# Two-layer RWKV and attention trunk: the token shift as one product on ScalarE and one multiply-add on VectorE, with two new terms in the planner's VectorE costs

## The chip, the cores and the metric

The program runs on one core of one Trainium2 chip. The metric is the device time of one execution in microseconds. The kernel before took 2802.55 us, the median of three runs (2799.92 to 2806.07).

## The reference

A sequence of 16 learned tokens and 1024 inputs (1040 tokens of width 1024, float32) passes through two layers, each a token mixer and a squared-ReLU MLP between normalizations. Layer 0's mixer is what the change touches. One matrix gives 18 tiles of 128 channels each: r, k and v of RWKV (tiles 0 to 11), the low-rank inputs for decay, rate and gate (12 and 13), and the input of a pooling mixer (14 to 17). Tiles 0 to 13 are shifted in time by a learned share mu of each channel:

```python
y = h @ w_in
ys = y[..., :SHIFT_WIDTH]
prev = jnp.pad(ys, ((0, 0), (1, 0), (0, 0)))[:, :L]
ys = ys + (prev - ys) * mu
...
o = rwkv7_scan(rf, dec, kf, vf, kk, a_h)     # S = S*w + sa (kk a) + v k, token by token
...
diffs.append((c - lag) / cnt - ug)           # moving averages of 2, 4, 8, 16 tokens
...
return jnp.concatenate([o, z], axis=-1) @ w_out
```

Layer 1's mixer is differential attention. It and both MLPs have the same instructions before and after.

## The kernel before, in words

**Stages.** Channels lie on the 128 partitions and tokens along the free axis, in three chunks of 348, 346 and 346 tokens. Each fp32 product is made as three fp32r matmuls of split operands (high by high, low by high, high by low; `mm3`, L363 to L370). The program is: an entry stage (normalization of the input, the projections of tiles 12, 13 and 4), the low-rank stage (`lora`), then a large planned stage with the rest of layer 0's mixer, then the output projection and MLP of layer 0 (`late`), attention, and the second `late`.

**The planned stage** lies between about 80 and 665 us. In it the code doesn't issue instructions; a `Recorder` takes each call down with the tiles it reads and writes (`call` and `keep`, L253 to L307), so every instruction of this stage has line L283 in the profile and is known by its tile names. `call` reckons a cost for each from the engine and the size (L263 to L281). `Flow.order` (L118 to L165) then walks through the tasks as a list scheduler: it keeps a clock for each engine, takes the engine that can start soonest, and on it the ready task with the longest chain of reckoned cost behind it. The result is one fixed order for each of the five queues (PE, VectorE, ScalarE, GpSimd, and SP, which issues the DMAs). On the chip each queue runs in that order, whatever the real durations are.

**What is planned.** For each of four pairs of heads p there is
- `proj`: the projections of the tiles that p needs, with the token shift (`project_c`), stored to DRAM (`yd`);
- `prep`: from these the operands of the chunked scan for 17 chunks of 64 tokens, in groups of two (tiles `q`, `w`, `zb`, `sa`, `sg`; two products called `pss` for norms), stored as `pk` and `ldd`;
- `invert`: 62 dependent VectorE operations on a 68-partition tile (`tm` and `raw`, in widths from 31 to 256 and back to 31), which invert the small triangular blocks of all 17 chunks at once. It loads its operands from `ldd` and an identity `eye`, and stores the result as `xd`, from which `ds` is loaded. All four inverts use the same `raw` tile, so one must have stored its result before the next may load;
- `chain`: the scan over the chunks, in groups of two. A group loads `lt` from `pk`, GpSimd builds `bd` from `ds` and `lt`, PE makes three products into `xs` with ScalarE (`x`, `gb`) and VectorE (`x`, `qq`, `mk`) between them, then the state `S` and the output `ob`; a finish with tiles `ft` writes the result to `ozd` or to `opa`.

Beside them stand `pool` (four moving-average mixers: GpSimd and VectorE on `u`, one product `ps<-u`, stored to `ozd`), `load` (reads `ozd` back and splits it into operands `opa`, one ScalarE cast and one VectorE subtraction per 260-token quarter) and `early` (the first six tiles of the output projection, 432 matmuls `ps<-opa,whi/wlo` of 260 columns, which need the loaded quarters). The list `PLAN` in which the generators are written down gives the order of recording, and so which buffer each takes; it is not changed.

**The token shift before.** `project_c` (L1127 to L1159) multiplies the PSUM sum by the row factor into `ys` on VectorE (L1153), with the last column of the chunk before in column 0. `shift` (L1161 to L1164) then makes the difference of the shifted and the unshifted view and a multiply-add, both on VectorE. Twelve tiles in three chunks go this way: three chunks in the entry stage and 33 in the planned one. `lora` also calls `shift`, for tiles 12 and 13 as a whole.

## Time and profile before

| | before |
|---|---|
| median of three runs | 2802.55 us |
| the profiled execution, its own time | 2802.57 us |
| its span | 2800.8 us |
| PE busy | 2597.9 us (93%) |
| VectorE busy | 2097.3 us (75%) |
| ScalarE busy | 1332.5 us (48%) |
| GpSimd busy | 302.4 us (11%) |

The span is the time from the first to the last instruction in the hardware profile; 1.8 us of the execution lie outside it. Times inside it are given from its start. A "row" is a line of one of the profile's views: a group of instructions by operation and shape, a stretch of the span with the busy time of each engine, a stretch of one engine's instructions in order of time, or who waited for whom. In timelines, square brackets hold the idle time just before an instruction and what ended it. PE is the matmul engine, DVE is VectorE, ACT is ScalarE, POOL is GpSimd. The row "PEclk" and the column of that name give the clock granted to the matmul engine, as a share of full speed.

### The profile page before, as it was taken

The numbers are of one execution on the slowest core, as the hardware profiler recorded it, in microseconds if no ns is written. First come the engines' busy times: TensorE is split into PE (matmuls) and PEld (weight loads), VectorE is DVE, ScalarE is ACT, GpSimd is POOL, SyncE is SP. The second block draws the span as 40 slices with busy tenths as digits, with TensorE's granted clock in tenths as the row PEclk, the third lists the DMA queues.
The fourth block names the chain that finished last, engine by engine and source line by source line (L and its number), as shares of the span: only waits on it lengthen the run. The fifth ranks groups of instructions, "written<-read, shape, count | busy, mean of one in ns | idle before, by whom it ended". The sixth has DMA issues, their size and how long they took to land.

```text
span 2800.8 us, 44525 instructions
## 1 busy us (share of the span) xinstructions
PE 2597.9 (93%) x16822; PEld 2359.1 (84%) x16822; DVE 2097.3 (75%) x3897; ACT 1332.5 (48%) x2727; POOL 302.4 (11%) x404
## 2 busy tenths in 40 slices
PE   7999988599999999999968999999899999999997
PEld 6889887499899999999957899988786788778877
DVE  5469778643987778887785888888648778778887
ACT  5456667243633335433343555655645333443342
POOL 0111333230000000000012232222000000000000
PEclk9999999699999999999988999999999999999998
DMA  4465676554333345443332222222243243544443
GB/s 152 168 204 187 211 222 216 146 162 169 137 114 126 147 177 205 168 137 130 96 127 68 69 64 79 63 67 61 76 160 129 105 165 141 196 174 137 149 160 119
DMA packets 180182, 391.16 MB, mean 140 GB/s; under 512 B 43104, under 2 KB 103904, under 8 KB 167552
## 3 DMA queue, kind: packets, MB, share of 16 engines
q1 hardware_dynamic: 152784, 348.14, 37.5%
q10 hardware_dynamic: 27184, 40.18, 4.1%
q8 instruction: 132, 2.16, 0.3%
q14 instruction: 82, 0.67, 0.1%
HBM read 240.17 MB, written 131.18 MB: 133 GB/s over the span
## 4 chain that ended last, share of the span: by engine, by line
PE 66%; DVE 9%; ACT 3%; issue 2%; DMA 2%; SPq 0%; POOL 0%; DVEq 0%; ACTq 0%
PE bank L681 46%; PE psq L368 2%; PE psq L369 2%; PE psq L370 2%; PE ps L283 2%; PE s L1777 1%; PE xs L283 1%; PE s L1779 1%; PE tr L1823 1%; ACT p L1796 1%; PE bank L723 1%; PE ob L283 1%; PE av L1849 1%; DVE p L1809 1%; DVE ac L758 1%
## 5 line engine op out<-in xcount | busy, mean ns | idle before, releaser
L681 PE MATMUL bank<-opa,wp 128*128 128x260 f32 (+1 forms) x3296 | 656.7, 319 | 6.9 <-DVE wp L772 3.5
L681 PEld LDWEIGHTS bank<-opa,wp 128*128 128x128 f32 x3296 | 517.0, 188 | 57.0 <-DVE wp L772 5.0
L681 PE MATMUL bank<-opb,wp 128*128 128x260 f32 (+1 forms) x1150 | 349.4, 325 | 3.0 <-DVE ac L991 3.0
L283 PE MATMUL ps<-opa,whi 128*128 128x346 f32 (+2 forms) x1008 | 267.9, 328 | 31.9 <-ACT opa L283 20.6
L681 PE MATMUL bank<-opa,hh 128*128 128x260 f32 (+1 forms) x1112 | 239.6, 320 | 7.2 <-DVE hh L772 5.3
L681 PEld LDWEIGHTS bank<-opb,wp 128*128 128x128 f32 x1150 | 217.4, 189 | 22.5 <-ACT opa L1014 3.4
L991 DVE TENSOR_TENSOR ac<-bank,ac 128x520 f32<-128x520 f32 (+1 forms) x256 | 171.1, 690 | 69.6 <-PE bank L681 67.7
L681 PE MATMUL bank<-opa,opb 128*128 128x260 f32 (+4 forms) x1168 | 203.7, 304 | 11.3 <-ACT opb L660 7.3
L283 PEld LDWEIGHTS ps<-opa,whi 128*128 128x128 f32 x1008 | 179.5, 191 | 34.5 <-ACT opa L283 21.1
L681 PEld LDWEIGHTS bank<-opa,hh 128*128 128x128 f32 x1112 | 184.7, 190 | 23.6 <-DVE hh L772 5.8
L681 PEld LDWEIGHTS bank<-opa,opb 128*128 128x128 f32 x1168 | 166.5, 192 | 22.3 <-ACT opb L660 7.7
L681 PE MATMUL bank<-opb,hh 128*128 128x260 f32 (+1 forms) x616 | 179.8, 325 | 0.0
L771 ACT CAST wp<-raw 128x512 fp32r<-128x512 f32 (+1 forms) x138 | 80.4, 584 | 196.7 <-PE bank L681 188.2
L283 PE MATMUL ps<-opa,wlo 128*128 128x346 f32 (+2 forms) x504 | 157.8, 313 | 0.0
L771 ACT CAST wp<-ss 128x512 fp32r<-128x512 f32 (+1 forms) x130 | 76.5, 589 | 165.5 <-PE bank L681 140.7
L1796 ACT ACTIVATE p<-s,m 128x272 f32<-128x272 f32 (+7 forms) x128 | 95.5, 751 | 86.1 <-DVE m L1792 84.4
L681 PE MATMUL bank<-opa,tt 128*128 128x260 f32 (+1 forms) x648 | 130.8, 319 | 2.2 <-ACT opb L1014 2.0
L681 PEld LDWEIGHTS bank<-opb,hh 128*128 128x128 f32 x616 | 116.9, 190 | 9.9
L368 PE MATMUL psq<-opa,wp 128*128 128x346 f32 (+2 forms) x352 | 118.1, 335 | 4.4 <-DVE rp L453 2.6
L353 POOL TENSOR_TENSOR wpx<-raw,wp 128x1024 fp32r<-128x1024 f32 (+1 forms) x14 | 33.9, 2424 | 789.5 <-PE bank L681 745.3
L370 PE MATMUL psq<-opa,wp 128*128 128x346 f32 (+2 forms) x352 | 113.8, 323 | 0.0
L681 PE MATMUL bank<-opb,opb 128*128 128x256 f32 (+4 forms) x456 | 111.4, 308 | 1.4 <-DVE tt L737 1.4
(398 smaller groups left out, 6567.6 us busy)
## 6 DMA issues: line engine op xcount, KB each, us to landing
raw<-in_w_dram SPq DMA_DIRECT2D x64, 1024.0 KB, 4.9
hid<-ac SPq DMA_DIRECT2D x14, 1820.0 KB, 5.8
hid<-ac SPq DMA_DIRECT2D x14, 1792.0 KB
hh<-hid SPq DMA_DIRECT2D x23, 1040.0 KB, 5.2
hh<-hid SPq DMA_DIRECT2D x23, 1024.0 KB, 6.8
pk<-sg ACTq DMA_DIRECT2D x32, 704.0 KB, 3.9
lt<-pk SPq DMA_DIRECT2D x32, 704.0 KB, 4.5
raw<-in_w_qkv_dram SPq DMA_DIRECT2D x24, 512.0 KB, 3.8
```

Of the source, the lines that this page charges most:

```text
L283: one = eng, cost, lambda: fn(*args, **kw), r, w
L353: (lo or nc.gpsimd).tensor_tensor(lw[:, :n], raw[:, :n], hi[:, :n].bitcast(F32), op=ALU.subtract)
L368: nc.tensor.matmul(ps, wh, xh, start=(first and i == 0), stop=False)
L369: nc.tensor.matmul(ps, wl, xh, start=False, stop=False)
L370: nc.tensor.matmul(ps, wh, xl, start=False, stop=(last and i == n - 1))
L681: nc.tensor.matmul(ps, use(x), use(y), start=start and i == j == 0, stop=i == len(ws) - 1 and j == 2, skip_group_check=not start)
L723: nc.tensor.matmul(acc, ones, use(src), start=first, stop=last)
L758: F.dve(NH, lambda mk=mk, k=k: stt(mk, mk, self.gcol(l, 1, k), y, op0=ALU.mult, op1=ALU.mult), r=nm + [("T", 2)], w=nm)
L771: F.act(n, lambda: nc.scalar.copy(use(t[0][:, :n]), src), r=rd, w=[z[0]] + claim)
L991: F.dve(NH, lambda d=d, q=q: tt(sv(d), q, sv(d), op=ALU.add), r=nq + nd, w=nd, ps=True)
L1777: nc.tensor.matmul(out(a, b), st[:, qs], kh[:, a:b], start=True, stop=False)
L1796: nc.scalar.activation(p[:, :L0], S[c][:, :L0], AF.Exp, bias=m2[:, c:c + 1], scale=0.125, accum_out=m2[:, 2 + c:3 + c])
```

## The change

Three edits.

1. In `project_c` the shift of a chunk becomes `z = (1 - mu) * y[1:]` on ScalarE, then `z = mu * y[:-1] + z` on VectorE. `shift` itself stays, for `lora`.
2. A 12-column tile `cmu` with 1 - mu is made once by one VectorE operation. It is a part of the tile `nkk`, whose name it has in the lists below.
3. In the planner's cost of a VectorE operation a `tensor_tensor_scan` is reckoned at 480 elements per us, the others at 960 as before, and 0.06 us is added when any operand is one column wide.

```diff
         elif eng == "DVE":
-            cost = n / 960 + .07 + (.06 if psum else 0.0)
+            cost = n / (480 if op == "tensor_tensor_scan" else 960) + .07 + (.06 if psum else 0.0) + (.06 if any(x.shape[-1] == 1 for x in aps) else 0.0)
...
         if shifted:
-            self.shift(y, mt, W, x[:, off:], x[:, off:])
+            z = x[:, off:]
+            nc.scalar.activation(z, y[:, 1:W + 1], AF.Copy, scale=self.cmu[:, mt:mt + 1])
+            nc.vector.scalar_tensor_tensor(z, y[:, :W], self.par[:, C_MU + mt:C_MU + mt + 1], z, op0=ALU.mult, op1=ALU.add)
...
-            nkk = self.yp.tile([P, 8], F32, name="nkk", bufs=1)
-            self.nkk, self.nka = nkk[:, 0:4], nkk[:, 4:8]
+            nkk = self.yp.tile([P, 20], F32, name="nkk", bufs=1)
+            self.nkk, self.nka, self.cmu = nkk[:, 0:4], nkk[:, 4:8], nkk[:, 8:20]
+            nc.vector.tensor_scalar(self.cmu, self.par[:, C_MU:C_MU + 12], -1.0, 1.0, op0=ALU.mult, op1=ALU.add)
```

Since the planner's costs change and one operation changes its engine, the order of the whole planned stage is a new one on all five queues; behind that stage the order is the same. Three places matter below.

The first is VectorE's queue at the last of the four inverts. Before, the invert's 62 operations (`tm` and `raw`) have only loaded quarters (`opa`) between them, and the first operations of chain 2 (`x_0` on its group `lt_0`, then `qq`, `mk`, and `x_1` of its next group) stand behind the invert's last row:

```order
L283 TENSOR_TENSOR tm_0_794<-raw_724 68x31
L283 TENSOR_TENSOR raw_724<-raw_724,tm_0_794 68x31
L283 TENSOR_TENSOR x_0_807<-lt_0_798,xs_0_803 128x128
L661 TENSOR_TENSOR opb_6261<-raw_724,opb_6261 128x768
L283 TENSOR_TENSOR qq_0_809<-lt_0_798,xs_1_804 128x128
L283 TENSOR_TENSOR mk_759<-lt_0_798,xs_1_804 64x2x64 x2
L283 TENSOR_TENSOR x_1_808<-lt_1_799,xs_0_803 128x256
L283 SCALAR_TENSOR_TENSOR u_2_820<-u_2_820,u_0_818 128x346
```

In the changed kernel the same four stand in the first third of the invert, the first of them behind its tenth operation:

```order
L283 TENSOR_TENSOR x_0_808<-lt_0_799,xs_0_804 128x128
L283 TENSOR_TENSOR opa_72<-yt_0_769,opa_72 128x260
L283 TENSOR_TENSOR tm_0_795<-raw_725 68x156
L283 TENSOR_TENSOR raw_725<-raw_725,tm_0_795 68x6x26
L283 TENSOR_TENSOR tm_0_795<-raw_725 68x175
L283 TENSOR_TENSOR raw_725<-raw_725,tm_0_795 68x7x25
L283 TENSOR_TENSOR tm_0_795<-raw_725 68x192
L283 TENSOR_TENSOR raw_725<-raw_725,tm_0_795 68x8x24
L283 TENSOR_TENSOR tm_0_795<-raw_725 68x207
L283 TENSOR_TENSOR qq_0_810<-lt_0_799,xs_1_805 128x128
L283 TENSOR_TENSOR mk_760<-lt_0_799,xs_1_805 64x2x64 x2
L283 TENSOR_TENSOR x_1_809<-lt_1_800,xs_0_804 128x256
```

Fifteen operations moved in this way from behind the invert into it: of chain 2's first two groups `x`, `qq` and two `mk` each and the four `ft` of its first finish, the last pool's `u`, and two more `opa`.

The second place is SP's queue ahead of that invert. Before, all its loads (`eye` and `ldd`, into `raw`) stand ahead of the four loads of the third invert's result (`ds_0`, which chain 2 needs):

```order
L283 DMA raw_724<-in_eye_dram 64x1024
L283 DMA raw_724<-ldd 16x32x32 x4
L283 DMA raw_724<-in_eye_dram 4x1024
L283 DMA raw_724<-ldd 1x32x32 x4
L283 DMA ds_0_795<-xd 32x16x32 x4
L283 DMA u_0_818<-yd 128x362
```

In the changed kernel they stand ahead of the invert's last five loads, and one quarter's load (`yt`) among the first ones:

```order
L283 DMA raw_725<-in_eye_dram 64x1024
L283 DMA raw_725<-ldd 16x32x32
L283 DMA yt_0_769<-ozd 128x260
L283 DMA raw_725<-ldd 16x32x32 x3
L283 DMA ds_0_796<-xd 32x16x32 x4
L283 DMA raw_725<-in_eye_dram 4x1024
L283 DMA raw_725<-ldd 1x32x32 x4
```

The `ds_0` loads moved up by two places of the queue.

The third place is ScalarE's queue at a pair of projected chunks (the first in the planned stage). Before, it holds the steps of `prep` alone; `q<-pss` is the logarithm of a norm:

```order
L283 ACTIVATE q_0_784<-yl_0_772,nkk 128x64
L283 ACTIVATE q_4_788<-pss_0_792,con 128x128
L283 ACTIVATE q_4_788<-q_4_788 128x128
L283 ACTIVATE sr_1_791<-q_4_788 128x128
L283 ACTIVATE sr_1_791<-yl_3_775,par 128x128
```

In the changed kernel the two products of the shift stand among them:

```order
L283 ACTIVATE q_0_785<-yl_0_773,nkk 128x64
L283 ACTIVATE yt_0_769<-ys_0_771,nkk 128x348
L283 ACTIVATE q_4_789<-pss_0_793,con 128x128
L283 ACTIVATE q_4_789<-q_4_789 128x128
L283 ACTIVATE sr_1_792<-q_4_789 128x128
L283 ACTIVATE yt_1_770<-ys_1_772,nkk 128x346
```

The norm's three steps now stand behind a product that waits for VectorE's `ys`.

## The prediction

> **What bounds the kernel now.** I read the page first: one number for the whole and the slices of the matmul engine.
>
> ```profile
> span 2800.8 us, 44525 instructions
> PE   7999988599999999999968999999899999999997
> PEclk9999999699999999999988999999999999999998
> ```
>
> PE is nearly full in nearly every slice of 70 us, so what counts is PE's idle time. The one deep hole of the planned stage is the eighth slice (490 to 560 us), where the granted clock sinks too. Next, the busy time by stretches of that stage:
>
> ```profile
> core 0: us, PE busy (x) PEld busy (x) DVE busy (x) ACT busy (x) POOL busy (x), PEclk, DMA share, GB/s
> 100.00:480.00 380.00, 346.55 (x2381) 327.31 (x2380) 285.74 (x860) 234.52 (x750) 100.92 (x183) 0.98 0.62 198
> 495.00:542.00 47.00, 15.09 (x73) 12.52 (x73) 32.86 (x89) 8.12 (x24) 8.94 (x12) 0.56 0.48 113
> 542.00:600.00 58.00, 53.55 (x426) 50.95 (x426) 27.52 (x69) 31.53 (x90) 17.47 (x23) 0.97 0.55 168
> 600.00:665.00 65.00, 65.00 (x551) 64.46 (x549) 24.82 (x56) 27.56 (x76) 16.00 (x18) 1.00 0.40 127
> ```
>
> From 100 to 480 us PE idles 33.5 us in 380, in many small waits; from 495 to 542 us it idles 31.9 us in one hole; then 4.5 us in 58, and none to the stage's end. So the stage ends when PE has done a fixed amount of work, and what an edit is worth is the PE idle time that it removes or makes. Whom PE waited for in the first stretch:
>
> ```profile
> PE sa L283 <- DVE sg L283: 10.3, 15, 1.4
> PE sp L283 <- DVE mk L283: 6.0, 4, 3.2
> PE sa L283 <- ACT sg L283: 3.5, 9, 0.9
> ```
>
> And in the hole, PE's timeline:
>
> ```profile
> 506.95 0.58 PE L283 MATMUL ps<-opa,whi 128*128 128x260 f32 x1 [12.08 <-ACT opa L283]
> ...
> 519.49 0.58 PE L283 MATMUL ps<-opa,whi 128*128 128x260 f32 x1 [8.51 <-ACT opa L283]
> ...
> 523.78 0.79 PE L283 MATMUL xs<-x,bd 128*128 128x128 f32 x2 [0.35 <-DVE tm L283]
> 530.29 0.77 PE L283 MATMUL xs<-lt,bd 128*128 128x128 f32 x2 [5.71 <-issue]
> ...
> 539.66 0.36 PE L283 MATMUL ps<-opa,whi 128*128 128x260 f32 x1
> ...
> 543.94 0.61 PE L283 MATMUL xs<-lt,bd 128*128 128x128 f32 x4
> ```
>
> Two kinds of work are left to PE there: `early` products, which wait for loaded quarters, and chain 2 (`xs`), of which only two steps run by 524.6 us. It is held by VectorE, whose timeline is:
>
> ```profile
> 502.57 0.19 DVE L283 TENSOR_TENSOR tm<-raw 68x31 f32<-68x31 f32 x1 [5.10 <-DMA raw<-ldd]
> ...
> 529.79 0.21 DVE L283 TENSOR_TENSOR raw<-raw,tm 68x31 f32<-68x31 f32 x1
> 529.91 0.27 DVE L283 TENSOR_TENSOR x<-lt,xs 128x128 f32<-128x128 f32 x1
> 530.11 0.95 DVE L661 TENSOR_TENSOR opb<-raw,opb 128x768 fp32r<-128x768 f32 x1
> 533.79 0.29 DVE L283 TENSOR_TENSOR qq<-lt,xs 128x128 f32<-128x128 f32 x1 [2.73 <-PE xs L283]
> 533.99 0.58 DVE L283 TENSOR_TENSOR mk<-lt,xs 64x128 f32<-64x128 f32 x2
> 534.71 0.42 DVE L283 TENSOR_TENSOR x<-lt,xs 128x256 f32<-128x256 f32 x1
> 535.05 0.51 DVE L283 SCALAR_TENSOR_TENSOR u<-u,u 128x346 f32<-128x346 f32 x1
> 536.70 0.17 DVE L283 SCALAR_TENSOR_TENSOR ft<-ob,ft 128x16 f32<-128x16 f32 x1 [1.14 <-ACT ft L283]
> 536.91 0.17 DVE L283 SCALAR_TENSOR_TENSOR ft<-ft,ft 128x16 f32<-128x16 f32 x1
> 537.12 0.23 DVE L283 SCALAR_TENSOR_TENSOR ft<-ob,par,ft 128x16 f32<-128x16 f32 x1
> 537.39 0.35 DVE L283 SCALAR_TENSOR_TENSOR ft<-ft,par,ft 128x16 f32<-128x16 f32 x1
> ...
> 539.50 0.85 DVE L283 TENSOR_TENSOR mk<-lt,xs 64x256 f32<-64x256 f32 x2 [0.21 <-PE xs L283]
> 540.38 0.42 DVE L283 TENSOR_TENSOR x<-lt,xs 128x256 f32<-128x256 f32 x1
> 540.72 0.41 DVE L283 TENSOR_TENSOR qq<-lt,xs 128x256 f32<-128x256 f32 x1
> ...
> 546.92 0.94 DVE L283 TENSOR_TENSOR opa<-yt,opa 128x260 fp32r<-128x260 f32 x2 [0.24 <-ACT opa L283]
> ```
>
> The last invert holds VectorE from 502.57 to 530.0 us. The `x` at 529.91 stands behind it, and PE's 530.29 follows from it: the 5.7 us that the row calls "issue" are the wait for the invert. The last pool's `u`, which unlocks further loads for `early`, stands behind it as well.
>
> **Term 1, the shift.** The rows of the operation that goes and of the nearest ScalarE operation of the same form (a scale by a column of `par`):
>
> ```profile
> L283 DVE TENSOR_TENSOR yt<-ys 128x346 f32<-128x346 f32 x22 | 11.9, 539 | 0.9
> L465 ACT ACTIVATE opa<-h,par x24: 568/571/583, 15.3 to 34.7; 128x346 fp32r<-128x346 f32 x16, 128x348 fp32r<-128x348 f32 x8
> ```
>
> 36 differences of 539 ns go: 19.4 us of VectorE. 36 products of 571 ns come: 20.6 us of ScalarE. The multiply-add stays, one small operation for `cmu` is added at the start, under the input's loads. Nearly all of it lies beside PE. In the entry stage three chunks are concerned; ScalarE and VectorE are both ahead of PE there, and I cost it at nothing (if the cover were gone, three times 0.57 us).
>
> In the planned stage 33 of each move. VectorE's load from 100 to 480 us sinks from 285.7 us by 33 times 0.539, 17.8 us or 6%; if PE's 16.3 us of waits for `sg` and `mk` sink by the same share, that is 1.0 us. ScalarE's load rises by 18.8 on 234.5 us, 8%; on the 3.5 us of waits for ScalarE's `sg` that is 0.3 us. A new wait comes with it: a product stands in ScalarE's queue until VectorE has made `ys`, and behind it stand norm steps and evictions (`q`, `sr`, `sg`, `zb`) for which VectorE and PE wait in turn. The bounds: each of the 19 waits for `sg` and `mk` shorter by one difference is 10.2 us of gain; each of the nine waits for ScalarE's `sg` longer by one product is 5.1 us of loss. I take 0.7 us of gain, near the middle, since the new order mixes both kinds of place.
>
> **Term 2, the new order at the last invert.** I take the invert's start as unchanged, 502.57 us. On SP the `ds_0` loads are moved ahead of the invert's last loads:
>
> ```profile
> 490.98 5.03 SPq L283 DMA_DIRECT2D raw<-ldd  x4
> 498.25 0.28 SPq L283 DMA_DIRECT2D raw<-in_eye_dram  x1
> 498.57 2.42 SPq L283 DMA_DIRECT2D raw<-ldd  x4
> 501.03 2.23 SPq L283 DMA_DIRECT2D ds<-xd  x4
> ```
>
> They take 2.23 us to issue, and SP had 2.24 us of idle time (496.01 to 498.25) where they now stand. So they cost nothing there, 2.2 us at most; and they land earlier for chain 2.
>
> The fifteen operations pulled into the invert lengthen it. From the rows above: 0.27 + 0.29 + 0.58 + 0.42 + 0.51 + 0.17 + 0.17 + 0.23 + 0.35 + 0.85 + 0.41 = 4.3 us, and two `opa` 0.9: together 5.2 us. Each could also make the invert wait for a step of PE or ScalarE. Before, 3.9 us passed from `x` to `qq`; now an `opa`, seven steps of the invert and their port waits lie between, some 4 us, so I put that at nothing, with 2 us as its bound. The invert then ends at 535.2 us instead of 530.0. Who waits for that: the store of the result and, behind it on SP, further quarters. Chain 3, which needs the result, comes long after in PE's order, so it costs nothing.
>
> Behind the invert stand two more `opa` (0.9 us) and then `x` of chain 2's third group, which ends at about 536.6 us. Before, that `x` ended at 540.8 us. From there to the fourth group's first product took 3.1 us (543.94), with the second group's `ob` and `sp` and three `early` products between; these are now done by then, which leaves about 1.7 us. So this product runs at 538.3 instead of 543.9 us: 5.6 us gained. By then the changed order has 30 `early` products ahead of it, the old one 21; at 65.00/551 or 118 ns each the nine are 1.1 us. From that place on PE has the same work to the stage's end, 118.6 of 123 us of it busy. Term 2 is 6.7 us of gain. Its bounds: with the 2.2 us on SP and the 2 us of waits, 2.5 us; if the 4.5 us that PE idled from 542 to 600 go as well, 11.2 us.
>
> **The clock in the hole.** After the restart at 530.29 us the matmuls are slow until the row at 539.66, that is for 9.4 us; the stretch was granted 0.56. The changed kernel fills the hole only thinly, so I take the same slow piece after its restart and no term for it. The Trainium skill (TensorE: Matmul & The Clock Gate, Part 1: The HAM clock gate) says that the clock falls to half after an idle window of about 3.4 us and comes back after about as long a busy one. The trace agrees with the half, but not with the short return, if the thin work from 530 us counts as busy. By that rule 6 of the 9.4 us would run at full speed, and the sum would be 3 us lower.
>
> **The sum.** The profiled execution took 2802.57 us, and the median of the runs before is 2802.55, so no correction is needed. 2802.6 - 0.7 - 6.7 = 2795.2; I forecast **2795 us**, 0.27% less. About 0.2%, or 5.6 us, is what a measurement of this kernel can tell from no change. The case's own range, from the bounds of term 2 and half those of term 1, is 2788 to 2802.
>
> **Rivals.** *The loads take the place of the invert.* Since the invert ends 5 us later, SP's store of its result stands 5 us longer ahead of the quarters behind it, and `early` starves after the restart: PE's idle time from 542 to 600 us grows by about what the hole loses. For it: the two long waits at 506.95 and 519.49 are for loaded quarters, not for chain 2. Against: more quarters now stand ahead of that store. It gives 2800 to 2803.
>
> *ScalarE's queue.* The 33 products wait for `ys`, and while one waits, the evictions behind it wait:
>
> ```profile
> L283 DVE TENSOR_TENSOR ys<-ps,rse 128x346 f32<-128x346 f32 x22 | 11.3, 512 | 20.3 <-PE ps L283 20.2
> ```
>
> VectorE itself idled 0.9 us before each of these `ys` for PE. A product placed too early holds ScalarE for that and its own 0.57 us, about 1.5 us. If 10 of the 33 hold an eviction that PE needs, 15 us come and the sum is 2810; it decides against the change from nine on, where the 7.4 us of gain and 5.6 us more are eaten up. For it: PE has only 9% of idle time there, and ScalarE is busy 62%. Against: the planner knows of the dependency and puts other work in front.
>
> *The order is better everywhere.* The reckoned costs are nearer to the real ones, and the hole closes further: by half of its 31.9 us. It gives 2786. For it: chain 2 has three groups free and the pool's `u` runs some 17 us earlier. Against: the quarters' loads are no faster.
>
> *The change moves only what had slack.* Then the hole's gain is lost again before 665 us, 2802; it is told from the first rival only by where PE idles.
>
> **How the numbers follow.** The forecast's case has 0.50, of which 0.36 lies below 2797 and 0.14 within 0.2%. The better order has 0.18 (faster); the two cases without an effect have 0.19 together (same); ScalarE's queue has 0.13, of which 0.12 is slower. That is faster 0.54, same 0.34, slower 0.12. The range of 8 in 10 leaves out the worse half of ScalarE's case and a third of the better order's: 2784 to 2807.
>
> **What would show it.** In the changed profile, VectorE's `x` of 128x128 should start at about 507 us, inside the invert; the invert should last about 33 us instead of 27.4; the fourth group's first `xs` should stand near 538 us; PE's idle time from 100 to 480 us should be 33 us give or take 5; the new ScalarE group `yt<-ys` should have 571 ns. I am wrong if that idle time moves by more than 10 us, if the invert starts more than 3 us later, or if PE has as much idle time from 495 to 600 us as before, 36.4 us.

## The result, and the profile after

The changed kernel takes 2811.93 us, the median of six runs (2808.15 to 2818.0), against 2802.63 for the kernel before (six runs, 2799.92 to 2806.07): a ratio of 1.0033 with a 95% interval of 1.002 to 1.0046. In a second set of runs (`after_again` below) it was 1.0024 (1.0014 to 1.0033). So it is slower by 7 to 9 us, where I had forecast 7.6 us less. The profiled execution is the slowest of the six, 2818.0 us with a span of 2816.2; as before, 1.8 us lie outside.

The first lines of the page, after:

```profile
span 2816.2 us, 44549 instructions
...
PE   7999888599999999999968999999899999999997
...
PEclk9999999699999999999988999999999999999998
```

The slices look as they did; a difference of 0.3% doesn't show in tenths. It has to be looked for between marks. Two marks are in both kernels: the last product of `prep` (`pss`), and the first product of the next stage (`bank`). PE's timeline of before:

```profile
494.48 0.38 PE L283 MATMUL pss<-sr,conb 128*128 128x128 f32 x2
...
666.01 3.86 PE L681 MATMUL bank<-opa,opb 128*128 128x260 f32 x30 [0.93 <-ACT yt L283]
```

And of after, with what PE does in the hole between the two:

```profile
505.38 0.49 PE L283 MATMUL pss<-sr,conb 128*128 128x128 f32 x2 [0.38 <-DVE bo L283]
...
517.80 0.80 PE L283 MATMUL xs<-lt,bd 128*128 128x128 f32 x2 [9.59 <-POOL bd L283]
...
550.76 0.59 PE L283 MATMUL ps<-opa,whi 128*128 128x260 f32 x1 [8.39 <-ACT opa L283]
...
558.65 1.06 PE L283 MATMUL xs<-lt,bd 128*128 128x128 f32 x4
...
677.00 3.89 PE L681 MATMUL bank<-opa,opb 128*128 128x260 f32 x30 [0.94 <-ACT yt L283]
```

The last `prep` product ends at 505.9 us instead of 494.9, the next stage begins at 677.0 instead of 666.0. The planned stage loses 11.0 us ahead of the first mark, and the way from there to the second is 171.1 us in both. The rest of the 15.4 us between the two spans, 4.4 us, lies behind the stage, where the instructions are the same; all 20 profiles of this study have 2134.8 to 2139.7 us there, so I count it as spread between executions. Each profile is one execution.

The busy time of both stretches, first of before, then of after (columns as in the prediction: PE, its weight loads, VectorE, ScalarE, GpSimd, granted clock, DMA share, GB/s). For after, the prediction's own stretches stand behind:

```profile
100.00:494.90 394.90, 359.76 (x2482) 339.29 (x2480) 297.26 (x892) 244.05 (x778) 105.07 (x188) 0.98 0.63 198
494.90:666.00 171.10, 133.73 (x1044) 127.93 (x1044) 85.20 (x213) 67.81 (x189) 43.12 (x54) 0.87 0.47 137
```

```profile
100.00:505.90 405.90, 362.80 (x2478) 340.85 (x2478) 286.63 (x860) 255.73 (x804) 103.44 (x190) 0.97 0.62 191
100.00:480.00 380.00, 340.61 (x2314) 321.43 (x2314) 262.71 (x784) 237.64 (x747) 93.21 (x176) 0.97 0.61 190
495.00:542.00 47.00, 30.88 (x163) 26.60 (x163) 32.70 (x89) 14.90 (x45) 15.33 (x19) 0.67 0.71 174
542.00:600.00 58.00, 44.25 (x327) 42.17 (x325) 33.95 (x88) 25.83 (x70) 13.53 (x17) 0.85 0.50 143
505.90:677.00 171.10, 140.85 (x1053) 134.97 (x1052) 84.93 (x215) 70.02 (x194) 43.86 (x54) 0.86 0.50 141
```

Up to the last `prep`, PE idles 43.1 us (405.90 less 362.80) where it idled 35.1, and is busy 3.0 us longer with the same matmuls. Behind it PE idles 30.3 us instead of 37.4 and is busy 7.1 us longer: the hole is emptier of idle time, as forecast, but no shorter. Whom PE waited for from 100 to 480 us, after (microseconds in total, number of waits, the longest):

```profile
PE sa L283 <- DVE sg L283: 9.8, 15, 2.7
PE ps L283 <- DVE ys L283: 7.1, 3, 3.0
PE sa L283 <- ACT sg L283: 6.3, 12, 1.2
PE sp L283 <- DVE mk L283: 3.1, 3, 2.1
```

The waits for `sg` on VectorE are what they were, although VectorE is busy 23 us less in this stretch (262.71 against 285.74; up to the last `prep` product, over the same work, it is 10.6 us, 286.63 against 297.26). Those for ScalarE's `sg` are 2.8 us longer, those for `mk` 2.9 us shorter. Over all rows of this view PE waited 11.2 us for ScalarE in both kernels, and 24.7 us for VectorE where it had been 19.8. The row for `ys` had 1.1 us before. In PE's timeline it is three long waits, each for an eviction that stood late in VectorE's queue:

```profile
224.28 0.66 PE L283 MATMUL ps<-opa,whi 128*128 128x346 f32 x1 [3.00 <-DVE ys L283]
...
296.87 0.85 PE L283 MATMUL ps<-u,pwt 128*128 128x348 f32 x2 [2.46 <-DVE ys L283]
...
312.30 0.42 PE L283 MATMUL ps<-opa,whi 128*128 128x346 f32 x1 [1.64 <-DVE ys L283]
```

VectorE at the last invert, after (the first row of the invert, the first `x` of chain 2, a wait inside the invert, the invert's last row, the `x` of the third group):

```profile
518.33 0.19 DVE L283 TENSOR_TENSOR tm<-raw 68x31 f32<-68x31 f32 x1 [3.49 <-DMA raw<-ldd]
...
522.97 0.27 DVE L283 TENSOR_TENSOR x<-lt,xs 128x128 f32<-128x128 f32 x1
...
533.72 0.85 DVE L283 TENSOR_TENSOR mk<-lt,xs 64x256 f32<-64x256 f32 x2 [2.00 <-PE xs L283]
...
553.27 0.21 DVE L283 TENSOR_TENSOR raw<-raw,tm 68x31 f32<-68x31 f32 x1
...
554.07 0.41 DVE L283 TENSOR_TENSOR x<-lt,xs 128x256 f32<-128x256 f32 x1
```

The chain's first steps are inside the invert, 4.6 us behind its start. But the invert starts 12.4 us after the last `prep` product (518.33 less 505.9), before 7.7. SP's queue shows what came in between:

```profile
504.65 0.74 SPq L283 DMA_DIRECT2D raw<-ldd  x1
505.48 0.84 SPq L283 DMA_DIRECT2D yt<-ozd  x1
509.48 1.38 SPq L283 DMA_DIRECT2D raw<-ldd  x3
510.90 2.10 SPq L283 DMA_DIRECT2D ds<-xd  x4
513.05 0.65 SPq L283 DMA_DIRECT2D raw<-in_eye_dram  x1
513.74 2.41 SPq L283 DMA_DIRECT2D raw<-ldd  x4
```

SP's idle time (506.32 to 509.48) now stands ahead of three of the first four `ldd` loads, not behind all four. So the four `ds` loads, 2.10 us, fall into no gap: they and the three late loads, 1.38 us, delay the invert's last loads. From the end of that idle time to the end of the last load's issue it is 6.7 us (509.48 to 516.15) where it was 2.7 (498.25 to 500.99), and this is most of the 4.7 us by which the invert starts later.

### The profile page after: what moved, and what is told of

Read it like the earlier page. It is cut to its first block, busy times and chain, and to the rows that moved or that the text cites. A ratio compares the mean times of both kernels' runs of the same rounds, so it can differ in the third digit from the quotient of the medians.

```text
span 2816.2 us, 44549 instructions
## 1 busy us (share of the span) xinstructions
PE 2614.5 (93%) x16822; PEld 2373.6 (84%) x16822; DVE 2084.2 (74%) x3862; ACT 1348.0 (48%) x2763; POOL 300.5 (11%) x404
## 4 chain that ended last, share of the span: by engine, by line
PE 66%; DVE 10%; ACT 3%; issue 2%; DMA 2%; SPq 0%; POOL 0%; DVEq 0%; ACTq 0%; POOLq 0%
PE bank L681 46%; PE psq L368 2%; PE psq L369 2%; PE psq L370 2%; PE ps L283 2%; PE xs L283 1%; PE s L1780 1%; PE tr L1826 1%; PE s L1782 1%; ACT p L1799 1%; DVE p L1812 1%; DVE opb L808 1%; PE bank L723 1%; PE ob L283 1%; PE av L1852 1%
## 5 line engine op out<-in xcount | busy, mean ns | idle before, releaser
L283 PE MATMUL ps<-opa,whi 128*128 128x346 f32 (+2 forms) x1008 | 277.3, 334 | 22.1 <-DVE ys L283 9.4
L681 PEld LDWEIGHTS bank<-opa,opb 128*128 128x128 f32 x1168 | 169.2, 195 | 22.5 <-ACT opb L660 7.9
L681 PEld LDWEIGHTS bank<-opa,tt 128*128 128x128 f32 x648 | 103.0, 189 | 12.0 <-issue 2.2
```

The source lines that it names most:

```text
L283: one = eng, cost, lambda: fn(*args, **kw), r, w
L681: nc.tensor.matmul(ps, use(x), use(y), start=start and i == j == 0, stop=i == len(ws) - 1 and j == 2, skip_group_check=not start)
```

## The experiments

The theory after this reading was that the new order makes the loss and not the work: any change to a planner's cost draws another order, and the one of before happens to be a good one. Its first rival was that the products on ScalarE hold its queue.

**Work and order apart.** `old_order` has the new operations at the places of the old ones (the product is planned as the subtraction was), `new_order` the old operations in the new order.

```diff
 # old_order, against before; the shift of the change, and in call():
+        if getattr(self, "as_dve", False): eng, cost = "DVE", n / 960 + .07
-        port = eng == "POOL" or eng == "DVE" and not psum and len(aps) > 2
+        port = eng == "POOL" or eng == "DVE" and not psum and (len(aps) > 2 or self.__dict__.get("as_dve", False))
 # new_order, against before; the planner's costs of the change, the old shift, and in call():
+        if eng == "DVE" and getattr(self, "as_act", False):
+            eng, cost, port = "ACT", n / 1200 + .18, False
```

> The 36 products run on ScalarE, but every instruction of the planned stage stands where it stood in the kernel before: the product is planned at the place and the cost that the subtraction had. Theory 'order': the 9.3 us that the change lost are lost by the new order, in PE's waits before the last prep ends (505.4 us after, 494.5 before); then this kernel has 2797 to 2804 us, the last prep ends at 493 to 496 us, and PE waits no longer for `ys` than before (1.1 us from 100 to 480). Theory 'ScalarE's queue': the products hold norm steps and evictions wherever they stand; then it has 2806 to 2815 us, and PE's waits for ScalarE's `sg` grow from 3.5 to 6 us or more.

> The subtraction runs on VectorE as before, but is planned as the product is (ScalarE's cost, the new costs of VectorE), so that nearly every instruction stands where it stands in the changed kernel. Theory 'order': it is at least as slow as the changed kernel, 2808 to 2822 us, since 17.8 us of work are back on VectorE, and the last prep ends at 503 us or later. Theory 'ScalarE's queue': without products on ScalarE the loss is gone, 2798 to 2804 us.

Measured: `old_order` 2812.64 us, 1.0025 (1.0012 to 1.0037); `new_order` 2814.76, 1.0028 (1.0018 to 1.0039). Each half alone costs what the whole costs. In the new order the loss needs no product on ScalarE at all. For `old_order`, though, theory 'order' had forecast 2797 to 2804 us and the last `prep` at 493 to 496, and it missed both (504.0). The time is that of 'ScalarE's queue', while PE's waits for ScalarE's `sg`, 5.6 us, stay a little under the 6 that this theory asked for. In the old order the product does hurt, where nothing was planned around it. VectorE's waits of `old_order`, 100 to 480 us:

```profile
DVE yt L284 <- ACT yt L284: 15.4, 16, 2.5
```

The multiply-add follows at once, and waits 15.4 us in 16 places for ScalarE. In after, the same multiply-adds wait 1.3 us in three places of that stretch. So the planner does its part: it hides most of that wait, and in doing so it draws another order.

**Each edit alone.** `shift_only` has the shift with the old costs, `costs_only` the costs with the old shift; `shift_scan`, later, has the shift and the scan's cost without the one-column term.

```diff
 # shift_only, against after
-            cost = n / (480 if op == "tensor_tensor_scan" else 960) + .07 + (.06 if psum else 0.0) + (.06 if any(x.shape[-1] == 1 for x in aps) else 0.0)
+            cost = n / 960 + .07 + (.06 if psum else 0.0)
 # costs_only, against after
-            z = x[:, off:]
...
+            self.shift(y, mt, W, x[:, off:], x[:, off:])
 # shift_scan, against after
-            cost = n / (480 if op == "tensor_tensor_scan" else 960) + .07 + (.06 if psum else 0.0) + (.06 if any(x.shape[-1] == 1 for x in aps) else 0.0)
+            cost = n / (480 if op == "tensor_tensor_scan" else 960) + .07 + (.06 if psum else 0.0)
```

> The shift as changed, the planner's costs as before (so the planner knows of the product on ScalarE, but not of longer scans and single columns). If the loss comes by the costs of the planner, this has 2796 to 2803 us; if it comes by the product's new place in the plan, 2808 to 2815 us. By a third theory, that any new order is a new draw of PE's waits, with a spread of some 10 us, it lies anywhere from 2795 to 2815 us and its waits stand at other places than in the changed kernel.

> The shift as before, the planner's costs as changed. If the loss comes by the costs, this has 2808 to 2815 us and the last prep ends past 503 us; if by the product's new place, 2798 to 2804 us. By the third theory (any new order is a new draw) it lies anywhere from 2795 to 2815 us, and the two parts alone do not add up to the whole.

> The changed kernel without the planner's 0.06 us for operands of one column: the shift on ScalarE and the scans at double length alone. With the columns' cost the ratio was 1.0024 to 1.0033, with neither planner cost 1.0016. If the loss is in the columns' cost, this has 1.0010 to 1.0018; if in the scans', 1.0024 or more; if only the draw counts, anywhere from 1.000 to 1.0035.

Measured: 1.0016 (1.0004 to 1.0029), 1.0029 (1.0017 to 1.004) and 1.0033 (1.0018 to 1.0048). No edit alone carries the loss, and they don't add up.

**Orders drawn anew with nothing else changed.** If the order is a draw, a cost changed by a hundredth of a microsecond must move the time as much as the change did. Four such against before, two against after:

```diff
 # n_act: ScalarE's fixed cost
-            cost = n / (1700 if psum else 1200) + (.2 if wide else .1) + (.08 if hasattr(kw.get("scale"), "ap") else 0.0)
+            cost = n / (1700 if psum else 1200) + (.2 if wide else .11) + (.08 if hasattr(kw.get("scale"), "ap") else 0.0)
 # n_pool, and after_pool against after: GpSimd's fixed cost
-            cost = n / 450 + .15
+            cost = n / 450 + .16
 # n_dve: VectorE's rate
-            cost = n / 960 + .07 + (.06 if psum else 0.0)
+            cost = n / 950 + .07 + (.06 if psum else 0.0)
 # n_hand, and after_hand against after: the time from one engine to another
-                ready[j] = max(ready[j], end + (0.0 if T[j][0] == e and not size else .3))
+                ready[j] = max(ready[j], end + (0.0 if T[j][0] == e and not size else .31))
```

> The kernel before, with one number of the planner's costs moved by next to nothing: ScalarE's fixed cost 0.11 instead of 0.1 us. No work is moved between engines; only the order is drawn anew (655 rows of difference on PE, where the changed kernel has 839). Theory 'content': the loss comes by what the change does (products on ScalarE, scans and columns at other costs); then this kernel is within 0.1% of before, 2800 to 2808 us. Theory 'the order before is a good draw': any new order of this planner costs PE some 5 to 10 us of waits before the last prep ends, so this one is 0.15 to 0.4% slower, and its last prep ends at 500 us or later.

> The same with another number: GpSimd's fixed cost 0.16 instead of 0.15 us (355 rows of difference on PE). By 'content' it is within 0.1% of before; by 'the order before is a good draw' it is 0.15 to 0.4% slower, with its PE waits at other places than those of the other new orders.

> A third neutral draw: the kernel before with VectorE reckoned at n/950 instead of n/960 (451 rows of difference on PE). By 'the order before is a good draw' it is 0.1 to 0.4% slower than before, and PE idles 40 us or more from 100 us to the last prep's end (35.1 before); by 'content' it is within 0.1% and idles 33 to 37 us.

> A fourth neutral draw: 0.31 instead of 0.3 us for a result handed from one engine to another (390 rows of difference on PE). The same two forecasts: 0.1 to 0.4% slower with 40 us or more of idle time, or within 0.1% with 33 to 37 us.

> A neutral draw of the changed kernel: 0.31 instead of 0.3 us for a result handed on, which on the kernel before gave the ratio 1.000. If the change costs something of its own, 0.1 to 0.2% stay whatever the draw: ratio 1.0015 to 1.0035. If only the draw counts, it lies anywhere in the neutral draws' 1.000 to 1.0035.

> A second neutral draw of the changed kernel: GpSimd's fixed cost 0.16 instead of 0.15 us, which on the kernel before gave 1.0035. The same two forecasts: 1.0015 or more if the change has a cost of its own, anywhere from 1.000 to 1.0035 if only the draw counts.

Measured, without the change: `n_act` 1.0011 (0.9999 to 1.0023), `n_pool` 1.0035 (1.0023 to 1.0047), `n_dve` 1.0015 (1.0006 to 1.0024), `n_hand` 1.0 (0.9986 to 1.0014). With it: `after_hand` 0.9988 (0.9978 to 0.9998), `after_pool` 1.0005 (0.9995 to 1.0016). Single forecasts were not all met: 'the order before is a good draw' asked for 0.15 to 0.4% from `n_act` and for 0.1 to 0.4% and 40 us of idle time up to the last `prep` from `n_dve` and `n_hand`. Only `n_pool` met it in full. `n_act` lies between the two theories, `n_dve` has the ratio but 37.7 us of idle time, and `n_hand` is as fast as before with 40.7 us. So before's order is a good one, but not the only good one. Orders with the change's work and orders without it cover the same ground, and the lowest ratio of these six has the work in it. The work of the change costs nothing that these runs can tell; the order that it happened to draw costs the 0.3%.

**The clock in the hole.** PE's granted clock in the hole is 0.6 in both kernels. To see what that costs, dummy products on PE (their result is overwritten or not read) keep it busy there.

```diff
 # after_spin, against after, the 56 (the 48 are put at a product ps in the same way; before_spin, against before, has 72 and 50 at two products ps)
+        spin = lambda: [self.real.tensor.matmul(idle[0], idle[1], idle[1], start=idle[3], stop=idle[3]) for _ in range(idle[2])] if idle else None
+        one = eng, cost, lambda: (spin(), fn(*args, **kw)), r, w
...
+                if (p, g0) in {(2, 0): 56}:
+                    nc.idle = xs[:, 0], cb[:, B_BLK:B_BLK + P], {(2, 0): 56}[p, g0], True
```

> The changed kernel in its own order, with products of constants added on PE that nobody reads, ahead of the two long waits of the hole: 56 ahead of chain 2's first product (9.6 us of waiting) and 48 ahead of the fifth step of the first early tile (8.4 us). Theory 'clock': in the hole the change does win its 7 us of PE idle time, but 28.1 us of PE's work there runs at half clock instead of 14.5; kept busy, PE stays at full clock, the work at half clock falls by 10 us or more, and the kernel gains 4 to 7 us, 2805 to 2808 us where the changed kernel has 2812. Theory 'the invert holds it': the hole ends with the loads and the invert whatever PE's clock is; then the time stays as that of the changed kernel within 2 us, or is up to 3 us longer for the added work.

> The kernel before in its own order, with 72 and 50 such products ahead of its two long waits for early products (12.1 and 8.5 us). By 'clock' the 14.5 us of work at half clock fall to 5 or less and it is 3 to 5 us faster than before; by 'the invert holds it' it is the same within 2 us.

> The changed kernel once more, beside the next one on the same chip, for a second profile of the same order. If the 43 us that PE idles from 100 us to the end of the last prep belong to its order, they are 40 to 46 us again (35 before) and the ratio is 1.002 to 1.0045; if they were an accident of one execution, they are nearer to 35 us and the ratio is under 1.002.

> The changed kernel with the 104 idle products in the hole, beside the changed kernel itself. By 'clock' it is 4 us or more (0.14%) faster than that one, with 11 to 12 us of work at half clock from the last prep to the stage's end instead of 28; by 'the invert holds it' the two agree within 2 us, and the hole is as long.

The first 59 us of the hole, of after and then of `after_spin`:

```profile
505.90:565.00 59.10, 31.53 (x134) 27.33 (x134) 38.10 (x101) 14.93 (x42) 12.36 (x16) 0.60 0.59 148
```

```profile
501.10:560.00 58.90, 50.52 (x363) 47.00 (x362) 39.23 (x105) 18.20 (x50) 12.61 (x16) 0.88 0.57 155
```

The clock rose from 0.60 to 0.88, in before's hole from 0.62 to 0.91. Measured: `after_spin` 1.0034 (1.0021 to 1.0047), `before_spin` 1.0001 (0.9992 to 1.0011). Run side by side with after itself once more: `after_again` 2813.74 us, 1.0024 (1.0014 to 1.0033), `after_spin_again` 2814.52, 1.0028 (1.0015 to 1.0041). In the profiles the way from mark to mark was some 3 us shorter in after's order (166.9 and 167.8 against 171.1 and 170.4) and the same in before's (170.9 against 171.1); the medians show no gain. So the 4 to 7 us of theory 'clock' are not there; in after's order a gain of up to 3 us is not excluded (the section on the prediction comes back to it).

**The three waits for `ys`.** They make up 6.0 us of the 8.0 us of new idle time. `after_ys` moves six `ys` seven to nine places forward in VectorE's queue and keeps everything else in its order.

```diff
 # after_ys, against after: in order(), on the finished list
+            q = {e: [i for i in out if T[i][0] == e] for e in free}
+            v = q["DVE"]
+            for k, m in {21: 8, 22: 9, 28: 7, 29: 7, 30: 8, 31: 8}.items():
+                at = v.index(soon[k])
+                v.insert(at - m, v.pop(at))
```

> The changed kernel with six instructions moved and nothing else: the six `ys` of VectorE for which PE waits 3.0, 2.5 and 1.6 us (at 224, 297 and 312 us of the profile after) stand 7 to 9 places earlier in VectorE's queue. Theory 'ys': these 7.1 us are most of the 8 us that PE idles more than before up to the last prep's end; then its idle time there falls from 42 or 43 to 35 to 38 us, the last prep ends 4 to 7 us earlier, and the kernel has 0.05 to 0.2% less than the changed kernel beside before (ratio 1.0005 to 1.0020). Theory 'the order sets the pace, not single places': what is saved at these places comes back at the next wait (for `sg`, `mk`, loads), idle time stays over 40 us and the ratio at 1.0024 to 1.0033.

Measured: 2814.44 us, 1.0026 (1.0016 to 1.0037), no gain. PE's waits for `ys` did go, from 7.1 to 0.9 us in the stretch to 480 us, but its idle time up to the last `prep` is 44.0 us (43.1 in after). PE's waits of `after_ys` at the places of the three long ones:

```profile
228.83 0.49 PE L297 MATMUL pss<-sr,conb 128*128 128x128 f32 x2 [2.18 <-DVE sr L297]
234.02 0.43 PE L297 MATMUL ps<-opa,whi 128*128 128x346 f32 x1 [0.94 <-DVE ys L297]
...
298.44 0.49 PE L297 MATMUL xs<-x,bd 128*128 128x128 f32 x2 [2.62 <-ACT x L297]
...
314.79 0.46 PE L297 MATMUL sp<-lt,mk 128*128 128x128 f32 x2 [1.82 <-DVE mk L297]
```

PE comes earlier to the next product and waits there for `sr`, `x` or `mk`, which the moved `ys` pushed back or which would not have been ready sooner anyhow; the runs don't tell these two apart. The longest waits in the list were where PE met a delay, not its source. This theory fell.

**The stage's two parts on purpose.** `after_hand` and `after_pool` gained in the way alone (161.5 and 158.1 us), with chain 2's steps spread through the whole last invert. The theory was that the end of the last `prep` and the way from there are set by separate pieces of the order. So `after_chain` raises the priority of chain 2 in after's planner, and `before_hole` does it in before's, with the loads of the stage's last part reckoned at 0.8 of their size. Both leave the order as it was up to the hole or shortly before it.

```diff
 # after_chain, against after (first: the tasks of chain 2); before_hole, against before, with 3 for 8
+        for i in getattr(self, "first", ()):
+            rank[i] += 8
 # before_hole as well (hole: the tasks of PLAN's last part)
+            if i in hole:
+                size *= .8
```

> The changed kernel with chain 2's steps given 8 us of priority in the planner. The order is that of the changed kernel up to the hole (the first moved row of PE is past the last prep); in the hole VectorE's third `x` of chain 2 no longer stands behind the last 37 steps of the invert, and `mk`, `qq` and two more groups follow inside it. Theory 'two terms': the time up to the last prep and the hole behind it are set by two separate pieces of the order; the last prep ends at 503 to 507 us as after, but from there to the next stage's first product it takes 158 to 165 us instead of 170 to 171, and the ratio is 0.999 to 1.001. Rival 'the order as a whole': what the hole saves is spent behind it (chain 3 and the early products wait for loads); it stays 168 us or more and the ratio at 1.0024 or more.

> The kernel before, its shift and its planner's costs, in its own order up to shortly before the hole; from the last stage's tasks on the planner reckons loads at 0.8 of their size and gives chain 2 3 us of priority, so that chain 2's steps are spread through the last invert instead of standing behind it. By 'two terms' it joins the early end of the last prep of the order before (493 to 498 us) to a short way from there (158 to 165 us instead of 171): the next stage begins at 652 to 662 us instead of 666, ratio 0.995 to 0.9985, faster than both kernels. By 'the order as a whole' it is anywhere from 0.999 to 1.0035.

Measured: `after_chain` 2809.11 us, 1.0012 (1.0001 to 1.0023); `before_hole` 2796.23 us, 0.9969 (0.9954 to 0.9983), faster than before, and so faster than after. The windows of `before_hole` between the same marks:

```profile
100.00:496.30 396.30, 359.62 (x2479) 339.43 (x2478) 294.28 (x890) 241.53 (x774) 107.38 (x189) 0.98 0.63 198
496.30:658.90 162.60, 139.14 (x1048) 131.58 (x1047) 87.84 (x215) 68.85 (x194) 43.27 (x53) 0.92 0.49 142
```

And its last invert with the `x` of chain 2:

```profile
503.95 0.19 DVE L293 TENSOR_TENSOR tm<-raw 68x31 f32<-68x31 f32 x1 [2.32 <-DMA raw<-ldd]
...
510.09 0.27 DVE L293 TENSOR_TENSOR x<-lt,xs 128x128 f32<-128x128 f32 x1
...
517.05 0.42 DVE L293 TENSOR_TENSOR x<-lt,xs 128x256 f32<-128x256 f32 x1
...
527.68 0.42 DVE L293 TENSOR_TENSOR x<-lt,xs 128x256 f32<-128x256 f32 x1 [0.51 <-PE xs L293]
...
536.81 0.41 DVE L293 TENSOR_TENSOR x<-lt,xs 128x256 f32<-128x256 f32 x1
...
543.78 0.41 DVE L293 TENSOR_TENSOR x<-lt,xs 128x256 f32<-128x256 f32 x1
...
549.14 0.22 DVE L293 TENSOR_TENSOR raw<-raw,tm 68x31 f32<-68x31 f32 x1
```

Five groups of the chain pass while the invert runs, which takes 45.4 us for it instead of 27.4; behind its end PE has no wait over 0.9 us up to the next stage. The last `prep` keeps the early end of before's order (496.3), and the way is 8.5 us shorter. Which of its two edits did it was not run. In `after_chain` the last `prep` stays late (507.3) and the way falls by 3.7 us, to 167.4. That lies between the two theories (158 to 165 us, or 168 and more), and so does the ratio. It is less than `after_hand` gained, whose steps are spread no deeper; why, I have not settled.

The marks of all kernels, in us, each from one profiled execution (two for after: the second is in brackets):

| kernel | ratio | last `prep` ends | way to the next stage |
|---|---|---|---|
| before | 1 | 494.9 | 171.1 |
| before_hole | 0.9969 | 496.3 | 162.6 |
| before_spin | 1.0001 | 494.5 | 170.9 |
| after | 1.0033 (1.0024) | 505.9 (504.8) | 171.1 (170.4) |
| after_hand | 0.9988 | 505.4 | 161.5 |
| after_pool | 1.0005 | 511.5 | 158.1 |
| after_chain | 1.0012 | 507.3 | 167.4 |
| after_ys | 1.0026 | 507.9 | 169.2 |
| new_order, old_order | 1.0028, 1.0025 | 506.8, 504.0 | 169.6, 169.8 |
| shift_only, costs_only | 1.0016, 1.0029 | 500.4, 506.9 | 172.1, 171.2 |
| shift_scan | 1.0033 | 502.5 | 173.3 |
| n_act, n_pool | 1.0011, 1.0035 | 508.5, 498.9 | 160.3, 173.6 |
| n_dve, n_hand | 1.0015, 1.0 | 500.7, 500.9 | 175.6, 167.2 |

Every order that differs from before's ahead of the hole ends its last `prep` 4 to 17 us later. (`old_order` is before's order with a slower chain in it.) But a late end is not yet a loss. The kernels with the latest ends (`after_pool`, `n_act`) have the shortest ways, and those with early ones (`n_pool`, `n_dve`) the longest. What counts is the sum of both columns, the start of the next stage: 667 to 678 us in these orders, 666.0 before. The change's order, with 677.0, is one of the slower ones.

## Why the prediction was wrong

The forecast was 2795 us: a gain of 0.7 us in the many small waits and of 6.7 at the last invert. The measured change is a loss of 7 to 9 us. Two terms failed, the first of them for the most part of the difference, and with them the premise under both. (The range of the case, from the bounds in the text, sums to 2786 to 2803 and not to 2788 to 2802; the measured time lies outside either, and outside 2784 to 2807.)

**Term 1 failed as a sum.** It scaled the waits of before by the load of the engine waited for, with bounds of 10.2 us of gain and 5.1 of loss. That reckons as if the waits stayed where they were. The step that was missing: before's order is one particular draw, and a new draw has other waits. Idle time up to the last `prep` went from 35.1 to 43.1 us, and its end from 494.9 to 505.9. From 100 to 480 us it was 39.4 us, outside the 33 give or take 5 that I expected, though not by the 10 us that I had set as a sign of being wrong; the sign that did come was the invert's start, more than 3 us later. That the loss comes with the order is shown: the old operations in the new order lose as much (`new_order`), so do the costs alone, and hundredths of a microsecond in unrelated costs lose 0 to 0.35%. Term 1's durations held: the group of the new operation is

```profile
L283 ACT ACTIVATE yt<-ys,nkk 128x346 f32<-128x346 f32 x22 | 12.7, 579 | 10.5 <-DMA yd<-yt 6.5 <-DVE ys L283 3.9
```

579 ns against 571 forecast. VectorE's load did not sink as reckoned. From 100 to 480 us it fell by 23.0 us and not 17.8, but since everything comes later there, that stretch holds less of the work. Up to the last `prep` it fell by 10.6 us only: the differences that went were 16.8 us of it, and the 186 rows of `tm` and `raw` in the three inverts took 72.3 us instead of 66.4.

**Term 2 was right in its mechanism, and wrong at the invert's start.** The `x` of chain 2 stands 4.6 us into the invert, forecast 4.4. But the fourth group's first `xs` comes 52.7 us after the last `prep` (558.65 less 505.9), forecast 43.4 (538.3 less 494.9). Of the 9.3 us between: the invert starts 4.7 us later, where I took "unchanged" and priced the moved `ds` loads at nothing; it is longer by 2.5 us than forecast (35.1 us against 32.6), nearly all of it idle time inside the invert, 2.0 us for PE's `xs` in the row at 533.72 and 0.4 us ahead of an `ft`, where the text put such waits at nothing with a bound of 2 us (VectorE's busy time in the invert grew by 5.3 us, as summed); from the third group's `x` to the fourth group's product it takes 4.2 us instead of 1.7; and 0.4 us come back between invert and `x`. Behind that product 3.7 us are won and not 1.1 (118.4 us to the next stage, before 122.1), which leaves the way at 171.1 us: all of the 6.7 us is gone. The bound of 2.2 us for the `ds` loads was in the text; what I did not see is that SP's idle time, which was to cover them, stands in the new order ahead of three other loads as well.

**The hole's idle time and its length are two things.** From 495 to 600 us PE idles 29.9 us (47.00 less 30.88, and 58.00 less 44.25), before 36.4: 6.5 us less, as I took for the gain. That sign was a poor one, since the hole begins 11 us later in after and the stretch doesn't hold the same work; but between the marks it is the same, 7.1 us less idle time. PE was busy 7.1 us longer instead: weighted with the granted clock, 14.0 us of its busy time went to a clock below 1.00 there, before 7.2. By the waits in the timelines, chain 2 and the loaded quarters set the end of the hole. So the premise failed that PE has a fixed amount of work and that an edit is worth the idle time that it removes. From 100 us to the next stage PE idles 73.3 us after and 72.5 before, 0.8 us more, and yet the next stage begins 11.0 us later: in the sum it is PE's busy time that grew, by 10.1 us with the same matmuls.

**No term for the clock: not refuted.** The dummy products brought the clock up, and the medians show no time won. The 3 us that the sum would have had by the Trainium skill (TensorE: Matmul & The Clock Gate, Part 1: The HAM clock gate) are not seen: in before's order they lie just outside the interval (0.9989 against 0.9992). In after's they can't be excluded: there four matmuls of the chain itself took 1.06 us (558.65) that took 0.61 before (543.94), and the way was some 3 us shorter in both profiles with the dummy products.

**The rivals.** *ScalarE's queue* gave 2810, near to what was measured, but its mechanism did not decide: `new_order` has no product on ScalarE and is as slow. PE's waits for ScalarE's `sg` did grow, by 2.8 us, but without any product there they are longer still (7.2 us in `new_order`), and its waits for ScalarE in sum are unchanged (11.2 us). The products themselves waited long. From ScalarE's waits in after, 100 to 505 us:

```profile
ACT yt L283 <- DVE ys L283: 24.6, 7, 6.8
```

That is 24.6 us in seven places, and yet PE's own waits for ScalarE did not grow by it. *The loads take the invert's place* gave no gain in the hole, and there is none; PE's idle time from 542 to 600 us did grow, from 4.5 to 13.8 us. But the store of the invert's result was not its cause: the wait for a quarter that ends at 550.76 was over before the invert was (553.48). *The change moves only what had slack* says the same of the hole, a gain that is lost again before the stage ends, and gives no loss ahead of it. *The order is better everywhere* had the wrong sign for this draw. No rival named what decided, an order that by the draw is worse ahead of the last `prep`.

**What stays open**: which rows of the order let before end its last `prep` 4 to 17 us earlier than the others. Removing the three longest waits for `ys` did not move it, and no run here isolates it.

## What to carry to other kernels

Where a planner turns costs into a fixed order, an edit has two effects: its own, and that of the new draw. Price the second by drawing some neutral orders; here they spread over 0.35%, and an edit worth 1 us can't be judged by one run of it. Judge the edit by several draws with it and without it, and then pick the best order as a separate step.

In such a stage look for marks that both kernels have, and compare the way between them. The mark to judge by is the one where the orders are alike again, here the start of the next stage. Idle time of the busiest engine is not the loss, and its longest wait is not the cause, until a run that removes it gets shorter.

## What the runs showed of the hardware that was not expected

After some waits of 2 to 3 us, PE's next matmuls run at half of the full clock. In after, around the wait that ends at 224.28 us:

```profile
223.30:230.10 6.80, 5.82 (x20) 5.82 (x21) 6.63 (x21) 3.09 (x8) 0.71 (x3) 0.50 0.08 30
```

Half of the 5.82 us of busy time is lost here, 2.9 us beyond the wait itself. Not every such wait does it. Of the six waits of 2 us or more in after from 100 us to the last `prep`, four have a granted clock of 0.50 to 0.54 in the 3 us behind them, and two (at 296.87 and 490.21) have 1.00; so has before's longest there, 3.23 us up to 406.40. What decides it, no run here shows. Ahead of the last `prep`, 1.8 of the 3.0 us by which PE was busier come from the clock (10.8 us of busy time lost to a clock below 1.00, before 9.0). As to the length of the piece, two of the activity windows of 3.4 us that the Trainium skill names (TensorE: Matmul & The Clock Gate, Part 1: The HAM clock gate) would be 6.8 us, by estimate. In the thinly filled hole the clock stays low for much longer (0.60 over 59 us), and there it costs nothing that the medians show.

Single VectorE operations of an invert can take five times their usual time: a `tm` of 68x247 took 2.01 us in after where the next `tm`, of 68x240, took 0.40 us. Beside the slow one GpSimd ran one long operation on two SBUF tiles:

```profile
463.12 2.01 DVE L283 TENSOR_TENSOR tm<-raw 68x247 f32<-68x247 f32 x1
...
472.66 0.40 DVE L283 TENSOR_TENSOR tm<-raw 68x240 f32<-68x240 f32 x1
```

```profile
463.01 1.85 POOL L283 TENSOR_TENSOR wlo<-raw,whi 128x768 fp32r<-128x768 f32 x1
```

The two end within 0.3 us of each other (465.13 and 464.86). That the one held the other is likely from this, but no run moved it away. Over the three inverts ahead of the last `prep`, slower rows of this kind come to 5.9 us more in after than before.
